# A hybrid encoder layer on one core: sample chunk at full height, paired index heads, low weight parts by an adding DMA, moved stores and fillers

## The chip, the core and the metric

The kernel runs on one core of a Trainium2 chip. Its engines run their own fixed instruction lists side by side and wait for one another through semaphores: TensorE (PE, matmuls; PEld is its weight load), VectorE (DVE), ScalarE (ACT), GpSimd (POOL) and SyncE (SP), which in this kernel issues every DMA before the change. The metric is the device time of one execution in microseconds, the median of the runs shown. Only time counts here; the results must match the reference within its tolerance.

## The reference

One layer of a streaming encoder is computed for two request groups that share all weights: 512 prompt frames and 64 sample frames (576 columns together), model width 1024.

```
mod = silu(c) @ w_ada + b_ada                      # 6 blocks of 1024: shift, scale, gate, twice
h = rms(x) * g * (1 + sc1) + sh1
q,k,v, qi,ki,wi, z, xBC, dt, gates = split(h @ w_in)
# branch A: indexer I[t,s] = sum_h wi[t,h] * relu(qi[t,h] . ki[s] / 8), 8 heads; top k keys; softmax attention
# branch B: causal conv on xBC, chunked scan (SSD, 8 groups of 4 heads), D skip, silu(z) gate, group RMS norm
g_attn, g_ssm = split(sigmoid(gates))
x = x + gt1 * ((g_attn * (oA @ w_branch_attn) + g_ssm * (oB @ w_branch_ssm)) @ w_out)
h2 = rms(x) * g_ffn * (1 + sc2) + sh2
x = x + gt2 * ((silu(gate) * up) @ w_down),   gate, up = split(h2 @ w_gate_up)
```

The sigmoid is computed as (1 + tanh(x / 2)) / 2. New keys, values, conv rows and scan states are outputs too.

## The kernel before, in words

Every product with a weight keeps float32 accuracy with three fast passes. A weight tile of 128 x 1024 numbers (512 KB) is loaded into `raw` (two buffers, `NRAW`), then `split` (line 539) makes a rounded high part `wh` on ACT and the rest, `wl = raw - wh`, on DVE (three buffers of each, `NWH`). The activations have such parts too (`hTh`, `hTl`), and TensorE adds high times high, high times low and low times high. One tile applied to all 576 columns is 48 matmuls of 288 columns. The weight tiles stand in one list, in the order of their use; `fetch` loads and splits them ahead of it, numbered j from 0.

The body `build` doesn't issue instructions; it records operations with their buffers. `Plan.order` (line 363) then lays all of them out with a list scheduler: each operation has a cost from `cost` (line 316) and a priority (its place in the program, shifted by `R.prio`), and for each engine the next ready operation of best priority is taken. What comes out is one fixed order for each engine, SP's DMA issues among them. All instructions are therefore recorded under one line of the profile, L490 (line 490 emits them), and are told apart by the names of their tiles.

The stages, in order:

- Start: `x` is loaded (`xt`), normalised and transposed (`xnT`), while modulation blocks 0 to 3 of `w_ada` (`ada_pair`, tiles `adr`) give shift and scale. `h_tile` makes `hTh` and `hTl`. A second set of transposes makes `xs`, a copy of x in the other layout, stored to `x_d` and read again only after the output projection (lines 815 to 832).
- Small columns: `misc` (index keys, head weights `wi`, dt), the `e` chain of softplus for dt, cumulative sums `acs`.
- Index (line 1090): for each block of query rows, `kis` and `qis` give a score for each head, ACT applies relu (tile `lg`), DVE adds it up with the head's weight (`score`), then picks the top keys with 16 or 18 rounds of `max` and `match_replace`. The sample block (64 rows) runs 8 heads times two halves of 288 keys.
- Attention, for each of 4 key heads: logits `S` (`kst`, `qst`), softmax `P`, its transposes, the values (`pth`, `ptl`, `vst`). Between them TensorE runs fillers: 32 weight tiles of the gate and z columns that need nothing but `h`. `FILL` (line 612) says how many are recorded after each key head, `FILL0` how many before the first. A gate filler applies tanh, then `sg * 0.5 + 0.5` on DVE, and stores it to `gate_d`.
- SSD (line 1383): for each of 8 groups four weight tiles of x, B, C, a conv on DVE and ACT, then four prompt chunks of 128 steps and one sample chunk of 64. In `chunk`, `dec` (decay times CB) and `xdt` (dt times x) give the inside of the chunk and `cs` with the state `st` (tile `hst`) the outside; both add into halves of the array, 64 columns each, chosen by `tile_position` (line 1294). Modulation blocks 10 and 11 (`ada`, tiles `adr`, four loads of 512 KB each) are computed in the last group.
- Branch projections with their gates, modulation blocks 4 to 9 on DVE (`ada_columns`, `aacc`), output projection with `residual` and its gate `gt1`, the FFN by a Strassen-like scheme, the down projection.

```
        vec.tensor_tensor(lo, raw, hi.bitcast(F32), OP.subtract)          # split
    FILL = [6, 5, 5, 4]
            sync.dma_start(x_d[:, :, tb // 2, tb % 2 * P:tb % 2 * P + P], st)
            pe.matmul(o, xdt[:L, 64 * h:64 * h + 64], dec[:L, h, :L], start=True, stop=st is None,
                      tile_position=(0, 64 * (h % 2)))
                ada(10 + i, sd, 2)                                        # in group 7, i = 0 and 1
```

Of the kernel before, what the change touches and what calls it, by code (L numbers as in the profile page):

```python
# [9 lines left out]
OP = mybir.AluOpType  # L10
# [158 lines left out]
class Op:  # L169
    __slots__ = ("eng", "fn", "args", "kw", "dur", "dur_dma", "deps", "succ", "left", "prio", "pools", "t0", "t1", "i", "bytes", "mm", "slack", "port")  # L170
# [58 lines left out]
class Plan:  # L229
# [10 lines left out]
    def __init__(self, tc):  # L240
        self.tc, self.nc = tc, tc.nc
        self.ops, self.events, self.offset, self.slack = [], [], 0, SLACK
        self.vec, self.act, self.pool, self.pe, self.sync = (Engine(self, e) for e in ("vector", "scalar", "gpsimd", "tensor", "sync"))
# [21 lines left out]
    def add(self, eng, fn, args, kw):  # L265
        op = Op()
        op.eng, op.fn, op.args, op.kw = eng, fn, args, kw
        op.i, op.succ, op.pools, op.bytes, op.mm = len(self.ops), [], set(), 0, False
        op.prio = op.i - self.offset
        outs = [args[0] if args else kw["out"]]  # L270
        if kw.get("accum_out") is not None:
            outs.append(kw["accum_out"])
        outs = [o for o in outs if isinstance(o, View)]
        ins = [a for a in list(args[1:]) + [v for k, v in kw.items() if k not in ("out", "accum_out")] if isinstance(a, View)]
        deps = {}
        for v in ins:
# [6 lines left out]
        op.port = eng == "gpsimd" and wide > 0 or eng == "vector" and wide > 1  # L283
        op.dur, op.dur_dma = self.cost(op, outs, ins)
        self.ops.append(op)
        return op
# [29 lines left out]
    def cost(self, op, outs, ins):  # L316
# [10 lines left out]
        if e == "tensor":  # L327
# [8 lines left out]
            if op.kw.get("tile_position") is not None:  # L336
                return (73 if o.shape[0] <= 32 else 8 + n) / 1e3, 0.10
            return ((4 * max(n, 128) / 2.4 if n > 1 else 190) + 5) / 1e3, 0.10
        psum = any(is_psum(v) for v in ins)
# [23 lines left out]
    def order(self):  # L363
# [18 lines left out]
        def enable(op):  # L382
# [4 lines left out]
            t = 0.0  # L387
# [26 lines left out]
        while n < len(ops):  # L414
# [32 lines left out]
            if best == "sync":  # L447
                queue = max(at, queue) + 0.46
                dma_free = max(queue + 1.3, dma_free) + op.bytes / 360e3
                op.t1 = dma_free + op.dur_dma  # L450
            else:
                op.t1 = at + op.dur
# [45 lines left out]
def build(tc, I, O):  # L498
# [40 lines left out]
    def split(raw, nk, n):  # L539
# [5 lines left out]
        vec.tensor_tensor(lo, raw, hi.bitcast(F32), OP.subtract)  # L545
# [19 lines left out]
    def fetch(done, limit=1 << 30):  # L565
# [6 lines left out]
        with R.prio(4000 if done or limit > 99 else 0):  # L572
            more = True
            while more:
                more = False
                j = state["ld"]
                if j < min(len(queue), limit) and j < state["sp"] + NRAW:
# [6 lines left out]
                    else:  # L584
                        raws[j] = (load_raw(*s), s[1], s[2])
# [26 lines left out]
    FILL = [6, 5, 5, 4]  # L612
# [206 lines left out]
    with R.prio(-1500):  # L819
        for tb in range(5):  # L820
# [115 lines left out]
    def fillers(n, pl=None, bufs=2):  # L936
        for nf in range(len(nfs), len(nfs) + n):
            nfs.append(nf)
            if nf == 1 and n == NE:
# [8 lines left out]
                vec.tensor_scalar(sg, sg, 0.5, 0.5, op0=OP.mult, op1=OP.add)  # L948
# [3 lines left out]
            with R.prio(4000):  # L952
# [3 lines left out]
                if nf < 16:  # L956
                    vec.tensor_scalar(sg, sg, 0.5, 0.5, op0=OP.mult, op1=OP.add)
# [19 lines left out]
    vec.tensor_scalar(wi, misc[:, :, 64:72], float(NIH ** -0.5), None, op0=OP.mult)  # L977

# [111 lines left out]
    for b in (4, 1, 2, 3):  # L1090
# [5 lines left out]
        for h in range(NIH):  # L1096
            q0 = 8 * NP_ + h * NS if smp else h * NP_ + b * P
            q = qis[:, q0:q0 + rows]
            for c0, cn in (((0, TH), (TH, TH)) if smp else ((0, n),)):
                ps = px(f"pix{b}_{h}_{c0}", "py")  # L1100
                for a in range(2):
                    pe.matmul(ps[:rows, :cn], q, kis[:, a, k0 + c0:k0 + c0 + cn], start=(a == 0), stop=(a == 1))
                r = ap_.tile([P, NP_], F32, name=f"relu{b}_{h}_{c0}", tag="lg", bufs=4)
                sv = s[:rows, c0:c0 + cn]
                act.activation(r[:rows, :cn], ps[:rows, :cn], AF.Relu, scale=float(HD ** -0.5))
                if h == 0:
                    vec.tensor_scalar(sv, r[:rows, :cn], wi[:rows, b, h:h + 1], None, op0=OP.mult)
                else:
                    vec.scalar_tensor_tensor(sv, r[:rows, :cn], wi[:rows, b, h:h + 1], sv, op0=OP.mult, op1=OP.add)
        if not smp:  # L1110
# [151 lines left out]
    def chunk(g, c, xb, st):  # L1262
# [7 lines left out]
        dec = sd.tile([P, 4, P], F32, name=nm + "dec", tag="dec", bufs=2)  # L1270
# [10 lines left out]
        xdt = sd.tile([P, 256], F32, name=nm + "xdt", tag="xdt", bufs=2)  # L1281
# [42 lines left out]

    xbs, sts = {}, {}
# [57 lines left out]
    for g in range(NG):  # L1383
# [11 lines left out]
        for i in range(4):  # L1395
# [7 lines left out]
            if g == NG - 1 and i < 2:  # L1403
                ada(10 + i, sd, 2)
# [12 lines left out]
    for a in range(8):  # L1417
# [3 lines left out]
        with R.prio(4000):  # L1421
            vec.tensor_tensor(t2(g), ps, t2(g), OP.mult)
# [16 lines left out]
    for a in range(8):  # L1439
# [5 lines left out]
        vec.tensor_tensor(t2(g), ps, t2(g), OP.mult)  # L1445
# [28 lines left out]
    def residual(a, ps, hf, last):  # L1474
        x = x2[a][:, hf]
        for s, c0, n in SEG:
            vec.scalar_tensor_tensor(x[:, c0:c0 + n], ps[:, c0:c0 + n], gt1[:, a, s:s + 1], x[:, c0:c0 + n], op0=OP.mult, op1=OP.add)
# [16 lines left out]
    vec.tensor_scalar(gt2h, gt2, 0.5, None, op0=OP.mult)  # L1494
    for hf in range(2):
# [275 lines left out]
```

## Time and profile before

| | |
|---|---|
| runs, us | 1444.67, 1446.85, 1447.4 |
| median, us | 1446.85 |
| profiled execution, us | 1454.0 |
| its span, first to last instruction, us | 1452.3 |
| mean granted TensorE clock | 0.993 |

The profile is of one execution. Times are microseconds from the start of the span. "Busy" of an engine is the time in which one of its instructions ran; for PE the ends of pipelined matmuls are modelled, so the pace is better read from the distance of starts. A group's row has the busy time and the mean of one instruction, a window's row the busy time of each engine in a stretch. In a timeline or a wait table, the bracket or the arrow names how long the engine stood idle and what ended it. A matmul in plain float32 shows as two rows, one in the fast three-pass form as one.

### The profile page before, as it was taken

Reading aid. Unit: us, or ns where it says so; the run is one execution under the profiler, and the core shown is the slowest. Engines: PE = TensorE matmul, PEld = TensorE weight load, DVE = VectorE, ACT = ScalarE, POOL = GpSimd, SP = SyncE. Lnnn points to the kernel's source line nnn. Section 1 sums busy time; section 2 is a strip of 40 time slices with the busy share of each in tenths; the row PEclk is TensorE's granted clock in tenths of the full one; section 3 lists DMA queues with packets and bytes.
Section 4 is the critical chain, followed back from the end, with each engine's and each line's share of the span. In section 5 each row is a group of like instructions: output and inputs, shape, how many; then the busy total and the mean of one; then the engine's idle time right before and its main releaser. Section 6 shows DMA issues by size and latency. Waiting matters only on the chain.

```text
span 1452.3 us, 27797 instructions
## 1 busy us (share of the span) xinstructions
PE 1415.3 (97%) x10865; PEld 1339.4 (92%) x10865; DVE 1078.2 (74%) x2123; ACT 705.2 (49%) x1482; POOL 211.1 (15%) x320
## 2 busy tenths in 40 slices
PE   7999999999999899999999899999999999999998
PEld 5889999999999699999998699999999999999998
DVE  4468999887877777778777578984699888874221
ACT  5335233556556656555555441123566666663221
POOL 1211001210200144444444210000000000000000
PEclk9999999999999999999999999999999999999999
DMA  9822346333332434344333857775513333324331
GB/s 281 227 73 76 84 112 163 94 84 89 109 92 77 129 99 108 100 112 111 84 88 96 280 171 238 230 229 170 165 44 102 88 99 92 102 70 137 112 107 28
DMA packets 262356, 179.73 MB, mean 124 GB/s; under 512 B 24272, under 2 KB 239472, under 8 KB 262224
## 3 DMA queue, kind: packets, MB, share of 16 engines
q1 hardware_dynamic: 262224, 177.95, 42.7%
q8 instruction: 85, 1.39, 0.4%
q14 instruction: 47, 0.39, 0.1%
HBM read 153.09 MB, written 24.83 MB: 123 GB/s over the span
## 4 chain that ended last, share of the span: by engine, by line
PE 84%; DVE 8%; DMA 5%; SPq 1%; ACT 1%; issue 1%; DVEq 0%; ACTq 0%
PE mm L490 60%; PE py L490 15%; PE px L490 8%; DMA adr<-in_w_ada 2%; DMA raw<-in_w_in 2%; DVE aacc L490 1%; SPq L490 1%; DVE wl L490 1%; DVE m L490 1%; DVE score L490 1%; DMA xt<-in_x_sample 1%; ACT wh L490 0%; DMA x2r<-x_d 0%; DVE P L490 0%; DVE e L490 0%
## 5 line engine op out<-in xcount | busy, mean ns | idle before, releaser
L490 ACT ACTIVATE wh<-raw 128x1024 fp32r<-128x1024 f32 (+2 forms) x159 | 156.6, 987 | 279.9 <-PE mm L490 222.4
L490 DVE TENSOR_TENSOR wl<-raw,wh 128x1024 fp32r<-128x1024 f32 (+1 forms) x137 | 169.0, 1236 | 100.6 <-ACT wh L490 97.8
L490 PE MATMUL mm<-hTl,wh 128*128 128x288 f32 (+1 forms) x1024 | 235.0, 304 | 0.0
L490 PE MATMUL mm<-hTh,wh 128*128 128x288 f32 (+1 forms) x1024 | 230.6, 302 | 1.7 <-ACT xc L490 1.5
L490 PE MATMUL mm<-hTh,wl 128*128 128x288 f32 (+1 forms) x1024 | 232.1, 301 | 0.0
L490 PEld LDWEIGHTS mm<-hTh,wh 128*128 128x128 f32 (+1 forms) x1024 | 166.7, 189 | 5.4 <-ACT xc L490 1.8
L490 PEld LDWEIGHTS mm<-hTl,wh 128*128 128x128 f32 (+1 forms) x1024 | 167.4, 189 | 4.0 <-issue 1.9
L490 PEld LDWEIGHTS mm<-hTh,wl 128*128 128x128 f32 (+1 forms) x1024 | 167.3, 189 | 2.7 <-issue 0.5
L490 DVE SCALAR_TENSOR_TENSOR cu<-xc,wc,cu 128x579 f32<-128x579 f32 x96 | 82.9, 868 | 4.0 <-ACT cu L490 3.5
L490 PE MATMUL mm<-fl,wh 128*128 128x288 f32 x352 | 80.6, 298 | 1.0 <-DVE fl L490 1.0
L490 PE MATMUL mm<-fh,wl 128*128 128x288 f32 x352 | 80.1, 298 | 0.9 <-DVE x2r L490 0.9
L490 PE MATMUL mm<-fh,wh 128*128 128x288 f32 x352 | 80.0, 297 | 0.0
L490 PE MATMUL mm<-wh,hTl 128*128 128x256 f32 x256 | 73.2, 286 | 0.0
L490 PE MATMUL mm<-wh,hTh 128*128 128x256 f32 x256 | 72.8, 286 | 0.0
L490 PE MATMUL mm<-wl,hTh 128*128 128x256 f32 x256 | 72.7, 284 | 0.0
L490 DVE SCALAR_TENSOR_TENSOR aacc<-adr,sil,aacc 128x512 f32<-128x512 f32 x84 | 58.7, 747 | 2.9 <-DMA adr<-in_w_ada 2.7
L490 ACT ACTIVATE P<-lg,mn 128x128 f32<-128x128 f32 (+4 forms) x72 | 41.8, 582 | 39.1 <-DVE mn L490 38.3
L490 PEld LDWEIGHTS mm<-fh,wl 128*128 128x128 f32 x352 | 58.2, 189 | 1.6 <-DVE x2r L490 1.4
L490 PEld LDWEIGHTS mm<-fl,wh 128*128 128x128 f32 x352 | 58.2, 189 | 1.6 <-DVE fl L490 1.4
L490 PEld LDWEIGHTS mm<-fh,wh 128*128 128x128 f32 x352 | 58.1, 189 | 0.1
L490 PE MATMUL mm<-yh,wl 128*128 128x288 f32 x256 | 56.8, 302 | 0.0
L490 PE MATMUL mm<-yh,wh 128*128 128x288 f32 x256 | 56.5, 300 | 0.0
(409 smaller groups left out, 3771.0 us busy)
## 6 DMA issues: line engine op xcount, KB each, us to landing
raw<-in_w_in SPq DMA_DIRECT2D x80, 512.0 KB, 4.2
adr<-in_w_ada SPq DMA_DIRECT2D x48, 512.0 KB, 5.2
rawu<-in_w_gate_up SPq DMA_DIRECT2D x22, 512.0 KB, 3.9
raw<-in_w_gate_up SPq DMA_DIRECT2D x22, 512.0 KB, 3.9
bc<-acs_d SPq DMA_DIRECT2D x32, 256.0 KB, 3.6
raw<-in_w_branch_ssm SPq DMA_DIRECT2D x16, 512.0 KB, 4.9
raw<-in_w_down SPq DMA_DIRECT2D x16, 512.0 KB, 3.7
gate_d<-sg SPq DMA_DIRECT2D x16, 288.0 KB, 4.8
```

The costliest lines, as they stand in the source:

```text
L490: getattr(engines[x.eng], x.fn)(*[real(a) for a in x.args], **{k: real(v) for k, v in x.kw.items()})
```

## The change

Seven edits, made together:

1. Sample chunk: its `dec` and `xdt` get buffers of their own, `decS` and `xdtS`, whose rows 64 to 127 are set to zero once. The matmul reads all 128 rows in every chunk.
2. Index, sample block: heads 2h and 2h+1 stand beside each other in `qis`, so one matmul serves both, with 128 rows of result. Relu, weight and sum run on 128 rows, for 4 pairs. `wi2` holds the weights in that layout. At the end ACT copies the odd half, and DVE adds it.
3. Weight tiles j = 24 to 78 (from the fillers after the first key head to the last but one of the SSD): `wl` is written by ACT as minus `wh`, and a DMA issued by POOL adds `raw` onto it.
4. The store of `xs` is held back in the plan by 60 us.
5. The gates stay tanh: no `sg * 0.5 + 0.5`; the merge computes (g + 1) times the product, and `gt1h`, half of `gt1`, takes up the factor.
6. `FILL` is 5, 5, 5, 5. Modulation blocks 10 and 11 are recorded in SSD groups 2 and 3.
7. The planner's costs: an adding DMA has a price, sync transfers a lower rate, matmuls with a tile position 132 ns.

```diff
@@ order, add
+        op.hold = self.hold
-            t = 0.0
+            t = op.hold
@@ split
+        if not by_dma:
+            vec.tensor_tensor(lo, raw, hi.bitcast(F32), OP.subtract)
+        else:
+            act.activation(lo, hi.bitcast(F32), AF.Copy, scale=-1.0)
+            pool.dma_start(lo, raw, accum_op=OP.add)
@@ fetch
-                        raws[j] = (load_raw(*s), s[1], s[2])
+                        raws[j] = (load_raw(*s), s[1], s[2], 24 <= j < 79)
@@
-    FILL = [6, 5, 5, 4]
+    FILL = [5,5,5,5]
@@ x_d
+            R.hold = 60.0
             if tb < 4:
                 sync.dma_start(x_d[:, :, tb // 2, tb % 2 * P:tb % 2 * P + P], st)
...
+            R.hold = 0.0
@@ fillers (twice)
-                vec.tensor_scalar(sg, sg, 0.5, 0.5, op0=OP.mult, op1=OP.add)
@@ index
-        for h in range(NIH):
-            q0 = 8 * NP_ + h * NS if smp else h * NP_ + b * P
-            q = qis[:, q0:q0 + rows]
+        for h in range(NIH // 2 if smp else NIH):
+            q0 = 8 * NP_ + h * P if smp else h * NP_ + b * P
+            q = qis[:, q0:q0 + P]
+            w1 = wi2[:, h:h + 1] if smp else wi[:, b, h:h + 1]
...
+        if smp:
+            odd = ap_.tile([P, T], F32, name="odd", tag="lg", bufs=4)
+            act.activation(odd[0:NS], s[NS:P, :], AF.Copy)
+            vec.tensor_tensor(s[0:NS, :], s[0:NS, :], odd[0:NS], OP.add)
@@ chunk
-        dec = sd.tile([P, 4, P], F32, name=nm + "dec", tag="dec", bufs=2)
+        dec = decS if c == 4 else sd.tile([P, 4, P], F32, name=nm + "dec", tag="dec", bufs=2)
-        xdt = sd.tile([P, 256], F32, name=nm + "xdt", tag="xdt", bufs=2)
+        xdt = xdtS if c == 4 else sd.tile([P, 256], F32, name=nm + "xdt", tag="xdt", bufs=2)
-            pe.matmul(o, xdt[:L, 64 * h:64 * h + 64], dec[:L, h, :L], start=True, stop=st is None,
+            pe.matmul(o, xdt[:, 64 * h:64 * h + 64], dec[:, h, :L], start=True, stop=st is None,
@@ SSD loop
-            if g == NG - 1 and i < 2:
-                ada(10 + i, sd, 2)
+            if g in (2, 3) and i == 0:
+                ada(8 + g, sd, 2)
@@ branch merge (both branches)
-            vec.tensor_tensor(t2(g), ps, t2(g), OP.mult)
+            vec.scalar_tensor_tensor(t2(g), t2(g), 1.0, ps, op0=OP.add, op1=OP.mult)
```

More of the change, by code (lines that the diff above doesn't have):

```diff
@@ L169 @@
 class Op:
-    __slots__ = ("eng", "fn", "args", "kw", "dur", "dur_dma", "deps", "succ", "left", "prio", "pools", "t0", "t1", "i", "bytes", "mm", "slack", "port")
+    __slots__ = ("eng", "fn", "args", "kw", "dur", "dur_dma", "deps", "succ", "left", "prio", "pools", "t0", "t1", "i", "bytes", "mm", "slack", "port", "hold")
 class Pool:
@@ L977, in build @@
     vec.tensor_scalar(wi, misc[:, :, 64:72], float(NIH ** -0.5), None, op0=OP.mult)
+    wi2 = cp.tile([P, 4], F32, name="wi2")
+    for r in range(2):
+        vec.tensor_copy(wi2[64 * r:64 * r + 64], wi[0:NS, 4].rearrange("p (b r) -> p r b", r=2)[:, r])
     ki = misc[:, :, 0:64]
@@ L1323, in build @@
     so_s = O["ssm_sample"][0, 0].rearrange("h p n -> (h p) n").rearrange("(g a p) n -> g p a n", a=2, p=P)
+    decS = sd.tile([P, 4, NS], F32, name="decS")
+    xdtS = sd.tile([P, 256], F32, name="xdtS")
+    pool.memset(decS[NS:P], 0.0)
+    pool.memset(xdtS[NS:P], 0.0)
     xbs, sts = {}, {}
```

36 lines of the change are left out of this document (21 added, 15 removed).

## The prediction

> **What bounds the kernel now.** I read the page first, then the busy time by stage, then the chain of waits and the timeline at the places where TensorE loses time.
>
> ```profile
> span 1452.3 us, 27797 instructions
> PE 1415.3 (97%) x10865; PEld 1339.4 (92%) x10865; DVE 1078.2 (74%) x2123; ACT 705.2 (49%) x1482; POOL 211.1 (15%) x320
> ...
> PE 84%; DVE 8%; DMA 5%; SPq 1%; ACT 1%; issue 1%; DVEq 0%; ACTq 0%
> ```
>
> TensorE is busy for 97% of the span, and 84% of the chain that ends last lies on it. So only two things can shorten this kernel by much: TensorE work taken away, or one of its few gaps closed. The busy time by stage (windows: length, then PE, PEld, DVE, ACT, POOL, granted clock, DMA share, GB/s) shows where the gaps are.
>
> ```profile
> 0.00:36.00 36.00, 26.45 (x275) 20.75 (x276) 17.43 (x43) 18.65 (x33) 5.75 (x20) 0.95 0.92 281
> 36.00:110.00 74.00, 67.18 (x580) 62.94 (x579) 39.21 (x73) 25.99 (x49) 13.71 (x17) 0.98 0.53 149
> 110.00:460.00 350.00, 347.58 (x2574) 334.36 (x2574) 306.37 (x695) 178.08 (x374) 36.83 (x17) 1.00 0.37 100
> 460.00:500.00 40.00, 34.98 (x187) 26.98 (x186) 31.68 (x81) 23.85 (x58) 1.94 (x13) 0.91 0.22 62
> 500.00:797.00 297.00, 296.82 (x2333) 268.66 (x2332) 232.29 (x445) 174.08 (x426) 134.06 (x229) 1.00 0.40 107
> 797.00:815.00 18.00, 13.71 (x139) 10.43 (x139) 9.28 (x18) 7.30 (x16) 2.75 (x4) 0.91 0.87 277
> ```
>
> Length minus PE gives the idle time: 9.6 us in the first load, 6.8 up to 110, 2.4 in index and attention, 5.0 at the end of attention, 0.2 in the SSD, 4.3 at its end. The granted clock drops where TensorE idles: 0.91 of 40 us is 3.6 us more of lost pace, 0.91 of 18 us is 1.6, 0.98 of 74 us is 1.5.
>
> **Start: the copy of x stored later** (6 DMAs). SP's timeline, ACT's, DVE's and PE's:
>
> ```profile
> 43.39 9.27 SPq L490 DMA_DIRECT2D x_d<-xs  x6
> 58.99 1.00 SPq L490 DMA_DIRECT2D raw<-in_w_in  x2
> 60.57 0.23 ACT L490 ACTIVATE alg<-alg 128x32 f32<-128x32 f32 x1 [4.26 <-DMA alg<-in_a_log]
> 54.32 1.23 DVE L490 TENSOR_TENSOR wl<-raw,wh 128x1024 fp32r<-128x1024 f32 x1 [1.97 <-ACT wh L490]
> 55.80 1.23 DVE L490 TENSOR_TENSOR wl<-raw,wh 128x1024 fp32r<-128x1024 f32 x1 [0.25 <-ACT wh L490]
> ...
> 68.82 1.22 DVE L490 TENSOR_TENSOR wl<-raw,wh 128x1024 fp32r<-128x1024 f32 x1 [5.10 <-ACT wh L490]
> 61.16 0.28 PE L490 MATMUL px<-ident,lg 104*64 104x104 f32 x1 [3.10 <-ACT sg L490]
> ...
> PE px L490 <- DVE e L490: 2.5, 1, 2.5
> ```
>
> The stores hold SP for 9.27 us. Behind them in its queue stand the small tables and the next two weight loads (58.99). ACT waits for the table `alg`, and the gate tanh behind it is late: TensorE stands for 3.1 us. The weight lands late, DVE's `wl` at 68.82 waits, and the whole dt chain `e` stands behind that `wl`: TensorE waits 2.5 us more. Moved back, the stores come behind those tables and loads. Expected back: 3.1 + 2.5 and most of the 1.5 of clock, less what the next wait leaves, since SP gains at most 9.27 us and the two raw buffers are only free when DVE's `wl` ends at 55.6 and 57.0, so the loads come some 2 to 3 us earlier, and without the stores beside them. I take 5.5 us, between 2 and 8.3 (idle and clock together). The stores then stand ahead of later weight loads on SP; there the DMA engines are busy for 0.37 of the time and TensorE has the index's matmuls ready, so I cost that at nothing (without that cover up to the same 5.5, hence 0 in the lowest sum below).
>
> **Index heads paired.** 32 matmuls of 288 columns become 16:
>
> ```profile
> L490 PE MATMUL py<-kis,qis 128*64 128x288 f32 x32 | 6.5, 297 | 0.0
> 1158.33 4.83 PE mm L490 x36
> ```
>
> The pace in a steady stretch of the chain is 4.83 / 36 = 134 ns, so 16 x 0.134 = 2.1 us. DVE loses 8 sums and gains one, ACT loses 8 relus and gains a copy; TensorE doesn't wait for them there (2.4 us idle in 350).
>
> **Sample chunk at full height.** PE's timeline, a prompt chunk and a sample chunk:
>
> ```profile
> 814.22 0.45 PE L490 MATMUL py<-dec,xdt 128*64 128x128 f32 x4
> ...
> 815.29 0.70 PE L490 MATMUL py<-xw,bt 128*128 128x256 f32 x2
> 822.01 0.32 PE L490 MATMUL py<-dec,xdt 64*64 64x64 f32 x2
> 822.27 0.33 PE L490 MATMUL py<-cs,hst 128*64 128x64 f32 x2
> 822.53 0.33 PE L490 MATMUL py<-dec,xdt 64*64 64x64 f32 x2
> ...
> 824.07 0.53 PE L490 MATMUL mm<-oh,wl 128*128 128x288 f32 x2
> ```
>
> The prompt chunk does its 16 rows in 815.29 - 814.22 = 1.07 us. The sample chunk, with half the columns, needs 824.07 - 822.01 = 2.06. The difference between them is that `dec` there runs on 64 rows and `cs` on 128, in turn: each pair takes 0.26 us after the other, with nothing beside it. After the change both have 128 rows, and the two column halves can work side by side as in the prompt chunk. The changed program's order shows the 8 matmuls of every sample chunk still together, and none of 64 rows left. The cost then lies between 0.54 (half the columns, half the time) and 1.07 (time set by weight loads, not by columns); the row of the prompt chunk is the nearest, so I take 0.86. Gain: 8 x (2.06 - 0.86) = 9.6 us, between 7.9 and 12.2. The two clearing instructions on POOL come once.
>
> **Fillers 5, 5, 5, 5.** At the end of attention (460 to 500) idle and clock cost 8.6 us. In the old order the last 70 or so matmuls of the last key head stand with no filler between them; in the new one fillers run between them to the last, and 59 filler matmuls more are left for after it. One tile is 48 x 0.134 = 6.4 us of work that can fill. I take 6, between 0 (the chain of softmax is just as late) and 8.6.
>
> **Modulation blocks 10 and 11.** Chain of waits and PE's timeline:
>
> ```profile
> 800.49 6.79 DMA adr<-in_w_ada
> 802.49 0.79 PE L490 MATMUL mm<-oh,wh 128*128 128x288 f32 x4 [1.30 <-ACT oh L490]
> 807.33 1.08 PE L490 MATMUL py<-adr,sil 128*32 128x128 f32 x16 [2.99 <-DMA adr<-in_w_ada]
> ```
>
> Eight loads of 512 KB stand where the attention outputs, gates and branch weights are loaded too (DMA share 0.87). Moved to groups 2 and 3, they meet a share of 0.40. The 2.99 us go, the clock's 1.6 with them; the wait for `oh` may stay. I take 4.5, between 2 and 5.9. On SP the eight loads now stand ahead of weight loads of the SSD: two waits like the 2.99 would eat it all.
>
> **Tanh gates.** DVE loses 16 of these rows, and the merges keep their widths; `gt1h` is one small instruction.
>
> ```profile
> L490 DVE TENSOR_SCALAR sg<-sg 128x576 f32<-128x576 f32 x16 | 7.7, 479 | 6.7 <-ACT sg L490 6.7
> L490 DVE TENSOR_TENSOR wl<-raw,wh 128x1024 fp32r<-128x1024 f32 (+1 forms) x137 | 169.0, 1236 | 100.6 <-ACT wh L490 97.8
> L490 ACT ACTIVATE wh<-raw 128x1024 fp32r<-128x1024 f32 x128 | 135.2, 1059 | 251.9 <-PE mm L490 195.7 <-issue 40.6 <-DMA raw<-in_w_in 12.9
> raw<-in_w_in SPq DMA_DIRECT2D x80, 512.0 KB, 4.2
> o_d<-oT SPq DMA_DIRECT2D x4, 576.0 KB, 3.0
> x_d<-xs SPq DMA_DIRECT2D x4, 512.0 KB, 6.8
> ```
>
> **Low parts by adding DMA.** The new order has 55 of them. DVE loses 55 x 1.236 = 68 us and the 7.7 above; ACT gains 55 x 1.06 = 58. Both are off TensorE's path (DVE 306 of 350 and 232 of 297 us, ACT 178 and 174): by themselves worth nothing, beyond softmax answering sooner, which the fillers' term has. What counts is the weight feed. A raw buffer was held for load (4.2), ACT (1.06) and DVE (1.24), 6.5 us; now for load, two ACT passes and the adding DMA, and POOL and SP hold up what stands behind it (scan state, `dec`, `cs`; weight loads, `bc`). No adding DMA is in the trace. It reads two tiles and writes one, where a load reads one and writes one, so at the load's pace 4.2 x 1.5 = 6.3; at the least 3.0 (the store of a larger tile), at the most 6.8 + 4.2 = 11.0 (the slowest 512 KB row and a load). I take 6.3, which counts from the row nearest in size. Then a buffer turns in 4.2 + 2.1 + 6.3 = 12.6 us, a weight comes each 6.3 with two buffers; at the most each 8.7. TensorE uses one in 6.4 us when it runs tiles back to back, as at the start of the SSD, but on average one in 297 / 32 = 9.3 us there. So the feed holds on average, and is tight in runs of tiles. Loss: 3 us, between 0 and 4 tiles x (8.7 - 6.4) = 9.
>
> By the Trainium skill, page "DMA: Bandwidth & Descriptors", section "Anatomy of one DMA — SWDGE (gpsimd) path", a DMA issued by GpSimd takes about 2.0 us plus bytes over 436 GB/s, an estimate of 3.2 us here. With that the loss would be 0 and the sum 3 us lower. That fit is for plain copies, and no run here shows it yet.
>
> The planner's new costs reshuffle the order of every engine beside all this; where TensorE's idle is now 0.2 to 2.4 us in 300 it can win nothing and lose little, and I cost it at nothing.
>
> **Sum.** 5.5 + 2.1 + 9.6 + 6 + 4.5 - 3 = 24.7 us. Against the profiled execution's 1454.0 that is 1429.3; that execution is 7.15 above the median of 1446.85, and none of the terms depends on it, so the forecast for the median is **1422**. With all upper ends 8.3 + 2.1 + 12.2 + 8.6 + 5.9 = 37.1 it is 1410. With all lower ends and the full loss (0 + 2.1 + 7.9 + 0 + 2 - 9) it is 1444.
>
> **Rivals.**
>
> - *The gaps only move.* Matmul work goes (2.1 + 9.6 = 11.7), but what closes at one place opens at another: late weights hold the softmax tail and the SSD's start, since POOL's queue now has 55 DMAs that wait for ACT. For it: of all that SP waits for, DVE's `wl`, which frees a raw buffer, is the most, and there are still two raw buffers. Against it: idle in the SSD is 0.2 us in 297, with much slack on DVE and ACT. Time: 1446.85 - 11.7 = 1435. Chance 0.2.
>
> ```profile
> SPq L490 <- DVE wl L490: 494.1, 106, 23.4
> ```
>
> - *The pad does nothing.* If the 0.26 us of a pair comes from 64-column weight loads, not from the turn between 64 and 128 rows, 9.6 falls out: 1432. Against it: the prompt chunk's rows are of the same height and width of weights and run at half that. Chance 0.08.
> - *Weights starve (slower).* One mechanism: the adding DMA takes long enough that two raw buffers no longer feed TensorE. The point: 55 tiles, each (x - 9.3) late, eat the other 27.7 us at x = 9.8 us per weight, a buffer turn of 19.6, an adding DMA of 13.3. That is over twice my value and 2.3 above the dearest bound. At 16 us the turn is 22.3, the loss 55 x 1.85 = 102, the time 1446.85 - 27.7 + 102 = 1521; at 14, 1465. For it: every byte passes three times, beside loads and stores at 0.4 of the DMA engines. Against it: 512 KB rows of 3.0 to 6.8. Chance 0.1, at 1465.
>
> A rule speaks for this last one: the page "SBUF — State Buffer", section "SBUF: two separate sides", of the Trainium skill says that GpSimd can't write the entries of such a DMA while VectorE holds the port that they share, and a short DMA that took 0.62 us took 3.1 so. No run here shows it; 2.5 us more would leave the feed below the point.
>
> **How the numbers follow.** Forecast 0.62, with a range of its own of 1411 to 1433; gaps move 0.2; pad 0.08; starved 0.1. The first three are faster. A difference under 0.2% (2.9 us, the spread of the three runs being 2.7) can't be told from none. From the edge of the second I give 0.03 to no change: faster 0.87, same 0.03, slower 0.10. The range leaves out the starved case and about a tenth of the rest: 1408 to 1441.
>
> **What would show it.** Right: `py<-decS,xdtS` rows at under 0.9 us for a chunk; no 9 us of `x_d` stores ahead of the tables; PE idle near 2 us at the end of attention and at the SSD's end; `wl` landing 5 to 8 us after its issue by POOL. Wrong: PE waiting for a DMA into `wl` again and again, idle in the SSD above 10 us, or stores of x meeting the loads of the key and value weights.

## The result, and the profile after

| | before | after |
|---|---|---|
| median, us | 1446.68 | 1434.92 |
| runs, us | 1444.67, 1446.51, 1446.85, 1447.4 | 1429.4, 1434.5, 1435.34, 1436.43 |
| profiled execution, us | 1454.0 | 1434.5 |

A fourth run of the kernel before moves its median from 1446.85 to 1446.68. The ratio is 0.9914, with a 95% interval of 0.9886 to 0.9942: 12 us less, about half of the 24.7 us that the sum gave. The two profiled executions differ by 19.5 us, because that of before lies 7 us above its median; so stages are compared here for where they idle, and only runs for what a part is worth.

First the page of the changed kernel (busy time and share of each engine), then nearly the same stretches as before (length, then busy PE, PEld, DVE, ACT, POOL, granted clock, DMA share, GB/s).

```profile
span 1432.8 us, 27816 instructions
...
PE 1397.5 (98%) x10849; PEld 1330.7 (93%) x10849; DVE 1014.0 (71%) x2048; ACT 752.5 (53%) x1530; POOL 244.2 (17%) x377
```

```profile
0.00:36.00 36.00, 23.98 (x244) 18.62 (x248) 16.47 (x41) 17.03 (x31) 5.72 (x20) 0.95 0.91 270
36.00:110.00 74.00, 71.64 (x635) 67.20 (x635) 38.28 (x78) 29.85 (x60) 14.77 (x17) 0.98 0.56 154
110.00:440.00 330.00, 327.45 (x2428) 315.27 (x2427) 267.82 (x658) 195.45 (x391) 57.11 (x41) 1.00 0.55 137
440.00:500.00 60.00, 56.19 (x403) 53.97 (x402) 35.16 (x76) 39.02 (x84) 10.32 (x34) 0.99 0.68 175
500.00:797.00 297.00, 289.67 (x2386) 259.21 (x2387) 210.99 (x418) 192.00 (x437) 138.43 (x243) 0.98 0.66 159
797.00:815.00 18.00, 18.00 (x145) 15.70 (x145) 15.52 (x32) 9.30 (x21) 7.93 (x8) 0.93 0.80 271
```

Read length minus PE again. The last row idles nothing, because the SSD ends earlier here: TensorE's wait for `adr` (2.99 us) is gone, but that for `oh`, 1.30 us before, stays and now ends at 794.4 us, in the row above (TensorE's table of waits: what it waited for, us in total, times, longest).

```profile
PE mm L497 <- ACT oh L497: 1.6, 1, 1.6
```

In 36 to 110 us 2.4 us are idle instead of 6.8, but the first 36 us idle 12.0 instead of 9.6. The stretch of 500 to 797, most of the SSD, idled 0.2 us in 297 and now idles 7.3, at a clock of 0.98 instead of 1.00 (another 0.02 x 297 = 6 us of lost pace). The DMA share there rose from 0.40 to 0.66: the weight tiles pass through the DMA engines once more.

The gap at the end of attention is gone too, though the row of 440 to 500 doesn't say so: its 3.8 us are one later wait, which the same table names.

```profile
PE px L497 <- DVE xb L497: 5.0, 2, 3.8
PE px L497 <- DVE hst L497: 3.5, 3, 2.0
```

`xb` is the convolution's result and `hst` the scan state; both belong to the SSD, which so idles 3.8 + 7.3 = 11.1 us from 490 to 797. No row names a DMA into `wl`. The chain of waits, over the stretch that ends at the longest one, shows why (start, us, what; the second fence is a line of ACT's timeline):

```profile
473.66 7.31 DMA wl<-raw
480.97 0.02 SPq L497
...
481.02 8.02 DMA raw<-in_w_in
...
490.02 0.86 ACT cu L497
...
499.19 0.70 DVE xb L497
...
499.93 0.79 PE px L497 x2
```

```profile
489.06 1.06 ACT L497 ACTIVATE wh<-raw 128x1024 fp32r<-128x1024 f32 x1 [4.26 <-DMA raw<-in_w_in]
```

An adding DMA takes 7.31 us. Until then its raw buffer is in use, and SP can't issue the next weight load. That load takes 8.02 us, where the median of its kind is 4.2. On ACT the next instruction is `wh` of that weight, for which ACT stands idle for 4.26 us, and `cu`, the first pass of the convolution, stands behind it in the fixed order. So a late weight shows up as a late `xb`. In the SSD TensorE never waits for the weight itself.

What else the weight load met is in SP's timeline: right behind it stand the first two loads of a modulation block. The program before issues the first of them at the start of its SSD too (second fence; a load goes out as soon as its buffer is free, long ahead of its use), so it is the adding DMA that is new there. That it is the cause is argued here; the run with an eighth of its bytes, below, tests it.

```profile
481.02 0.37 SPq L497 DMA_DIRECT2D raw<-in_w_in  x1
481.44 1.58 SPq L497 DMA_DIRECT2D adr<-in_w_ada  x2
```

```profile
497.18 0.49 SPq L490 DMA_DIRECT2D adr<-in_w_ada  x1
```

The sample chunk did what it was to do. From the first of its 16 rows (8 matmuls in plain float32; some records are missing here) to the next work it needs 600.07 - 599.46 = 0.61 us instead of 2.06 (TensorE's timeline):

```profile
599.46 0.27 PE L497 MATMUL py<-cs,hst 128*64 128x64 f32 x1
599.47 0.27 PE L497 MATMUL py<-decS,xdtS 128*64 128x64 f32 x1
...
599.86 0.28 PE L497 MATMUL py<-cs,hst 128*64 128x64 f32 x2
600.07 0.70 PE L497 MATMUL py<-xw,bt 64*128 64x256 f32 x2
```

And the price of the adding DMA, from the DMA table (last number: median us from issue to landing) and the groups of instructions; the last row is of the kernel before:

```profile
wl<-raw POOLq DMA_DIRECT2D x55, 512.0 KB, 5.1
...
L497 POOL DMA_DIRECT2D wl<-raw x55 | 48.7, 886 | 221.1 <-ACT wl L497 159.4 <-PE py L497 27.0 <-ACT pth L497 18.7
L497 ACT ACTIVATE wl<-wh 128x1024 fp32r<-128x1024 f32 x55 | 58.2, 1061 | 0.2
L497 DVE SCALAR_TENSOR_TENSOR cu<-xc,wc,cu 128x579 f32<-128x579 f32 x96 | 91.9, 958 | 27.3 <-ACT cu L497 25.9
...
L490 DVE SCALAR_TENSOR_TENSOR cu<-xc,wc,cu 128x579 f32<-128x579 f32 x96 | 82.9, 868 | 4.0 <-ACT cu L490 3.5
```

The median of 5.1 us lies below the 6.3 that I took, and above the 3.2 of the fit on the page "DMA: Bandwidth & Descriptors", section "Anatomy of one DMA — SWDGE (gpsimd) path", of the Trainium skill; the measurement decides. DVE's `cu`, which had waited 4.0 us in all before (mean 868 ns), now waits 27.3 us, and takes 958 ns.

At this point my theory was: the gain is TensorE's work (pad and index) and the closed gaps, less 7 us and more in the SSD, lost because ACT's 55 additional passes push `cu` back.

### The profile page after: what moved, and what is told of

Its sections match the earlier page's. It is cut to its first block, busy times and chain, and to the rows that moved or that the text cites. A ratio compares the mean times of both kernels' runs of the same rounds, so it can differ in the third digit from the quotient of the medians.

```text
span 1432.8 us, 27816 instructions
## 1 busy us (share of the span) xinstructions
PE 1397.5 (98%) x10849; PEld 1330.7 (93%) x10849; DVE 1014.0 (71%) x2048; ACT 752.5 (53%) x1530; POOL 244.2 (17%) x377
## 4 chain that ended last, share of the span: by engine, by line
PE 84%; DVE 8%; ACT 2%; DMA 2%; issue 2%; POOL 1%; SPq 0%; ACTq 0%; DVEq 0%; POOLq 0%
PE mm L497 60%; PE py L497 15%; PE px L497 9%; DVE score L497 1%; DVE wl L497 1%; DVE m L497 1%; DVE cu L497 1%; DVE aacc L497 1%; DMA adr<-in_w_ada 1%; ACT wh L497 1%; DVE yl L497 1%; DMA raw<-in_w_in 1%; DMA wl<-raw 1%; DVE xb L497 0%; DVE tok L497 0%
## 5 line engine op out<-in xcount | busy, mean ns | idle before, releaser
L497 PE MATMUL mm<-hTh,wh 128*128 128x288 f32 (+1 forms) x1024 | 235.1, 305 | 1.7 <-ACT hTh L497 1.7
L497 PE MATMUL mm<-hTh,wl 128*128 128x288 f32 (+1 forms) x1024 | 235.4, 305 | 0.6 <-DVE wl L497 0.6
L497 PE MATMUL mm<-hTl,wh 128*128 128x288 f32 (+1 forms) x1024 | 231.8, 302 | 0.3 <-DVE hTl L497 0.3
L497 DVE TENSOR_TENSOR wl<-raw,wh 128x1024 fp32r<-128x1024 f32 (+2 forms) x82 | 98.8, 1207 | 79.0 <-ACT wh L497 76.2
L497 DVE SCALAR_TENSOR_TENSOR cu<-xc,wc,cu 128x579 f32<-128x579 f32 x96 | 91.9, 958 | 27.3 <-ACT cu L497 25.9
L497 POOL DMA_DIRECT2D wl<-raw x55 | 48.7, 886 | 221.1 <-ACT wl L497 159.4
L497 ACT ACTIVATE wl<-wh 128x1024 fp32r<-128x1024 f32 x55 | 58.2, 1061 | 0.2
```

The costliest lines, as they stand in the source:

```text
L497: getattr(engines[x.eng], x.fn)(*[real(a) for a in x.args], **{k: real(v) for k, v in x.kw.items()})
```

## The experiments

Each kernel was timed in five rounds beside the kernel before. "Worth" below is (1 - ratio) x 1446.68 us. In the diffs, `...` stands for lines left out here.

| run | kernel | median, us | ratio to before | 95% interval |
|---|---|---|---|---|
| (the change) | after | 1434.92 | 0.9914 | 0.9886 to 0.9942 |
| e1_no_dma | after, no adding DMA | 1428.07 | 0.9859 | 0.9833 to 0.9885 |
| e2_pad_only | before, pad alone | 1439.18 | 0.9938 | 0.9912 to 0.9965 |
| e3_hold_only | before, later stores alone | 1441.39 | 0.9955 | 0.9937 to 0.9973 |
| e4_dma_only | before, adding DMA alone | 1443.13 | 0.9967 | 0.9952 to 0.9983 |
| e5_dma_attention | after, adding DMA up to weight 47 | 1423.11 | 0.9833 | 0.9819 to 0.9848 |
| e6_act_pass | after, ACT's pass kept, DVE adds | 1441.38 | 0.9959 | 0.9946 to 0.9972 |
| e7_fill_ada | before, fillers and blocks alone | 1452.95 | 1.0044 | 1.0025 to 1.0062 |
| e8_no_hold | after, stores not held | 1432.39 | 0.9904 | 0.9887 to 0.9921 |
| e9_small_add | after, adding DMA of an eighth of the partitions | 1428.64 | 0.9866 | 0.9841 to 0.9892 |
| e10_old_fill | e5 with the fillers of before | 1419.72 | 0.9809 | 0.9785 to 0.9832 |
| e11_old_ada | e5 with the blocks in the last group | 1418.79 | 0.9802 | 0.9778 to 0.9825 |
| e12_both_old | e5 with both as before | 1418.78 | 0.9797 | 0.9778 to 0.9816 |

**No adding DMA.**

```diff
-                        raws[j] = (load_raw(*s), s[1], s[2], 24 <= j < 79)
+                        raws[j] = (load_raw(*s), s[1], s[2])
```

> The changed kernel, but every low part is made by DVE's subtraction, none by an adding DMA. Theory (the adding path's extra ACT passes, 55 x 1.06 us, stand ahead of the convolution's ACT work, so that xb and the scan state are late and TensorE idles 7.3 us in the SSD instead of 0.2): the SSD's idle falls below 2 us, ratio to the kernel before about 0.986 (1427 us), 6 to 9 us better than the changed kernel. Rival 1 (the adding path frees DVE, and that is what closed the gaps of attention): 0.995 or worse, with the gap at the end of attention back at 4 to 5 us. Rival 2 (the path is neutral, the missing gain is at the start): 0.991, as the changed kernel.

1428.07 us, 8 us better than the changed kernel: the adding DMAs cost more in sum than they win. The windows of this kernel, from its attention tail to its SSD, and TensorE's longest wait there:

```profile
443.00:500.00 57.00, 52.52 (x355) 48.82 (x353) 41.53 (x92) 35.27 (x85) 6.29 (x24) 0.97 0.40 121
500.00:785.00 285.00, 283.21 (x2402) 256.86 (x2400) 233.69 (x443) 170.18 (x412) 136.39 (x221) 1.00 0.42 113
```

```profile
PE px L497 <- DVE xb L497: 3.4, 1, 3.4
```

The gap of 4.5 us before the SSD is back, so rival 1 has a part in it. The 1.8 us of idle time in the SSD are the first half of one wait of 3.4 us for `xb`, from 783.2 to 786.6, which the end of the window cuts. So a late `xb` comes without any adding DMA too, and less of the SSD's loss goes with them than 7.3 - 1.8: from 490 to 815 us this kernel idles 4.6 us and the changed one 11.2. Which part of the path hurts this run doesn't say.

**The pad alone.**

```diff
+        dec = decS if c == 4 else sd.tile([P, 4, P], F32, name=nm + "dec", tag="dec", bufs=2)
...
+        xdt = xdtS if c == 4 else sd.tile([P, 256], F32, name=nm + "xdt", tag="xdt", bufs=2)
-            pe.matmul(o, xdt[:L, 64 * h:64 * h + 64], dec[:L, h, :L], start=True, stop=st is None,
+            pe.matmul(o, xdt[:, 64 * h:64 * h + 64], dec[:, h, :L], start=True, stop=st is None,
...
```

> The kernel before with the sample chunk's decay and input tiles padded to 128 rows, nothing else. Theory (11.1 us of TensorE work are taken away and nothing else moves): 0.9923 (1435.6 us), with the chunk's 16 rows at 0.66 us. Rival (gaps only move: TensorE waits elsewhere in the SSD for what the sample chunk's slowness hid): 0.996 or worse, idle in the SSD above 3 us. Rival of the pad (the time comes from 64-column weights, not from the turn between 64 and 128 rows): 16 rows stay at 2 us, 1.000.

Worth 9.0 us (5 to 13), against 8 x 1.45 = 11.6 from the rows above. TensorE's timeline and the window of the SSD in this kernel:

```profile
526.84 0.34 PE L490 MATMUL py<-decS,xdtS 128*64 128x64 f32 x4
...
527.50 0.70 PE L490 MATMUL py<-xw,bt 64*128 64x256 f32 x2
```

```profile
500.00:790.00 290.00, 287.85 (x2370) 263.09 (x2369) 236.17 (x447) 176.71 (x434) 131.49 (x227) 1.00 0.40 107
```

The chunk takes 0.66 us, so the rival of the pad falls. Of the other something is seen: 2.1 us idle in the SSD instead of 0.2, which is most of the difference between 11.6 and 9.0 (within the interval there need be none).

**The later stores alone.**

```diff
+            R.hold = 60.0
             if tb < 4:
...
+            R.hold = 0.0
```

> The kernel before with only the stores of the x copy planned 60 us later. My prediction's own term: 5.5 us, 0.9962 (1441.2 us). Theory now (the gap behind the tables closes, but the ada loads and the weights come no sooner, so the start's end hardly moves): 0.998 to 1.000, and the wait for alg gone from ACT's rows. Rival (the changed kernel's profile had a late start by chance): 0.996 with the first index matmul 5 us earlier.

Worth 6.5 us (4 to 9), so my theory of this run was wrong, and the prediction's 5.5 right. Its window from 36 to 110 us against the 6.8 us idle of before:

```profile
36.00:110.00 74.00, 73.14 (x641) 68.92 (x640) 41.94 (x85) 32.34 (x65) 14.91 (x17) 1.00 0.54 148
```

0.9 us idle, and the clock at 1.00 instead of 0.98.

**The adding DMA alone.**

```diff
+            act.activation(lo, hi.bitcast(F32), AF.Copy, scale=-1.0)
+            pool.dma_start(lo, raw, accum_op=OP.add)
...
-                        raws[j] = (load_raw(*s), s[1], s[2])
+                        raws[j] = (load_raw(*s), s[1], s[2], 24 <= j < 79)
...
```

> The kernel before with the adding DMA for the weights 24 to 78 and the planner's costs for it, nothing else. Theory (the SSD loses about 8 us to late conv results, attention wins a little from the freed DVE): 1.003 to 1.006 (1451 to 1455 us), idle in the SSD 5 to 10 us, waits of TensorE for xb and the scan state. Rival 1 (the freed DVE closes the attention gap and the SSD loss needs the other edits): 0.996 to 0.999. Rival 2 (neutral): 1.000. If weights starved, TensorE would wait for the DMA into wl: I expect no such row above 2 us.

4.8 us faster (2 to 7), where I expected slower: rival 1. The windows of this kernel, attention's end and the SSD:

```profile
450.00:490.00 40.00, 38.31 (x269) 36.06 (x268) 23.76 (x54) 26.80 (x59) 7.62 (x22) 1.00 0.65 165
490.00:780.00 290.00, 287.88 (x2255) 257.86 (x2255) 205.65 (x410) 190.76 (x432) 137.27 (x247) 1.00 0.65 153
```

At the end of attention it idles 1.7 us at full clock, where before it was 5.0 at 0.91, with the old fillers. So it is the adding path that closes that gap, not fillers. DVE's freed time is the likely reason: it is busy for 24 of those 40 us, where before it was 32. But this kernel has another order too, and no run parts the two. In the SSD it idles 2.1 us, less than my 5 to 10, and does 2255 matmuls in 290 us (7.78 a us) where before did 2333 in 297 (7.86): some 3 us lost by this rough count, since the two stretches mix the matmuls differently, and no starving.

**ACT's second pass without the DMA.**

```diff
             act.activation(lo, hi.bitcast(F32), AF.Copy, scale=-1.0)
-            pool.dma_start(lo, raw, accum_op=OP.add)
+            vec.tensor_tensor(lo, raw, lo.bitcast(F32), OP.add)
```

> The changed kernel where ACT still writes the negated high part (its second pass of 1.06 us stays), but DVE adds the raw weight to it in place of the adding DMA; so POOL issues nothing for it and DVE has its 55 passes back. Theory (ACT's extra pass ahead of the conv's ACT work makes the SSD late): the SSD still idles 5 us or more, 0.991 or worse. Rival (the DMA itself, its issue on POOL and its landing 5.1 us later, makes it late): the SSD's idle below 2 us, 0.987 or better.

The time fits my theory, but the place is wrong. The windows of this kernel, attention's end and the SSD:

```profile
460.00:508.00 48.00, 39.69 (x200) 29.94 (x199) 32.34 (x79) 27.84 (x64) 4.40 (x20) 0.89 0.29 88
508.00:785.00 277.00, 276.06 (x2332) 248.78 (x2332) 223.38 (x428) 185.87 (x430) 118.77 (x217) 1.00 0.42 116
```

In the SSD ACT is as busy as in the changed kernel (186 us in 277, against 192 in 297), and TensorE idles 0.9. So ACT's passes by themselves do not delay the SSD, in the order that this kernel has: the theory falls there. With DVE loaded again, and its subtraction now behind two ACT passes, attention idles 8.3 us at a clock of 0.89.

**The adding DMA in attention only.**

```diff
-                        raws[j] = (load_raw(*s), s[1], s[2], 24 <= j < 79)
+                        raws[j] = (load_raw(*s), s[1], s[2], 24 <= j < 48)
```

> The changed kernel with the adding DMA kept for the weights 24 to 47 (used in index and attention) and DVE's subtraction for the rest (SSD). Theory (the path helps in attention, where DVE is busy for 306 of 350 us, and hurts in the SSD): the best of these kernels, 0.984 to 0.987 (1424 to 1428 us). Rival (it hurts or is neutral in both): no better than the same kernel without any adding DMA. Rival (the SSD's loss is from other edits): 0.991 with the SSD's idle still above 5 us.

1423.11 us: 11.7 us better than the changed kernel (0.9914 - 0.9833), 3.8 better than with no adding DMA at all (though these two intervals overlap a little). The first 210 us from the SSD's start show it: of the changed kernel, then of this one.

```profile
490.00:700.00 210.00, 203.01 (x1692) 181.26 (x1692) 144.53 (x287) 137.32 (x311) 96.47 (x177) 0.98 0.71 172
```

```profile
490.00:700.00 210.00, 210.00 (x1793) 189.98 (x1792) 169.19 (x320) 124.78 (x302) 97.63 (x163) 1.00 0.44 119
```

7.0 us idle and 0.02 x 210 = 4.2 us of lost pace in one, nothing in the other: about 11 of the 11.7 us, given a clock of two digits. In the 100 us after them the two idle nearly alike, 4.2 and 3.2 us. This kernel has an order of its own, so these 11.7 us are the adding DMAs of the SSD together with the order laid out for them.

**The stores not held.**

```diff
-            R.hold = 60.0
+            R.hold = 0.0
```

> The changed kernel with the stores of the x copy planned where they were. My prediction's term: 5.5 us worse than the changed kernel, 0.9952. Theory now (the start won nothing, its gap moved to the next late load): 0.991 within 0.0015, with the 9 us of stores back ahead of the tables and TensorE's wait for sg back.

0.9904, the same as the changed kernel. Its SP timeline, one line of the changed kernel's for comparison (second fence), and its window:

```profile
47.51 5.06 SPq L497 DMA_DIRECT2D x_d<-xs  x4
54.64 0.35 SPq L497 DMA_DIRECT2D cs<-in_rope  x1
...
61.90 0.37 SPq L497 DMA_DIRECT2D raw<-in_w_in  x1
...
64.48 1.51 SPq L497 DMA_DIRECT2D x_d<-xs  x2
```

```profile
54.23 0.34 SPq L497 DMA_DIRECT2D cs<-in_rope  x1
```

```profile
36.00:110.00 74.00, 71.95 (x638) 67.30 (x637) 39.53 (x79) 30.41 (x61) 15.83 (x17) 0.98 0.55 155
```

I had expected the stores and the wait back; instead the plan puts two of the six behind the weight loads by itself, and 2.0 us idle, about as in the changed kernel (2.4). The other four still stand ahead of the tables (`cs`, the first of them), but they end at 52.57, before the tables go out. Without them, in the changed kernel, the tables go out at 54.23 all the same, where the kernel before had 52.76. So the stores no longer hold the tables, and the edit is worth nothing beside the other edits. Which of those delays the tables was not tried.

**Fillers and modulation blocks alone.**

```diff
-    FILL = [6, 5, 5, 4]
+    FILL = [5, 5, 5, 5]
-            if g == NG - 1 and i < 2:
-                ada(10 + i, sd, 2)
+            if g in (2, 3) and i == 0:
+                ada(8 + g, sd, 2)
```

> The kernel before with only the fillers 5, 5, 5, 5 and the two modulation blocks moved into groups 2 and 3. My prediction's terms: 6 + 4.5 = 10.5 us, 0.9927 (1436.3 us). Theory now (both gaps close): 0.991 to 0.995, with idle below 2 us at the end of the SSD and below 3 at the end of attention. Rival (the closing of attention's gap in the changed kernel came from DVE freed by the adding DMA, not from the fillers): 0.997, the attention gap still 4 us or more.

6.4 us slower (4 to 9), where prediction and theory had it faster. The windows of this kernel, end of attention and end of the SSD:

```profile
460.00:504.00 44.00, 37.24 (x169) 26.49 (x168) 32.35 (x95) 25.86 (x66) 1.11 (x10) 0.84 0.14 40
...
800.00:815.00 15.00, 12.23 (x92) 10.95 (x91) 11.92 (x21) 8.69 (x18) 2.75 (x6) 0.98 0.50 132
```

At the end of attention 6.8 us idle and 0.16 x 44 = 7.0 lost in pace make 13.8, against 8.6 before (in 40 us). One filler tile fewer after the first key head did not help the last one: TensorE still waits there for the parts of the softmax (`pth` 2.0 us, `mn` 1.1, `P` 0.9). At the end of the SSD 2.8 us idle instead of 4.3, with hardly any loss of clock.

**An eighth of the adding DMA, all else in place.**

```diff
-            pool.dma_start(lo, raw, accum_op=OP.add)
+            pool.dma_start(lo[:16], raw[:16], accum_op=OP.add)
```

> The changed kernel with every instruction in the same place on every engine, but each of the 55 adding DMAs treats 16 of the 128 partitions, an eighth of the bytes. Left out: the other 112 partitions of these low parts, so they hold the negated high part and the products are not the reference's. It divides what the adding path costs in the SSD. Theory (the transfer itself: its bytes beside the other DMAs, its landing of 5.1 us, its hold on DVE's rows): TensorE's idle in the SSD falls from 7.3 to below 3 us, DVE's cu rows from 0.98 to 0.90 us or less, time 1427 to 1430 us, as the kernel without adding DMAs in the SSD. Rival 1 (POOL's queue: 55 issues of 0.886 us and their waits for ACT, which an eighth of the bytes keeps): idle stays at 6 us or more if the issue time stays near 0.9 us, 1433 to 1436 us. Rival 2 (the order that the planner makes for it): the same, 1433 to 1436 us, even where the issue gets shorter.

Neither clean case. The time is that of the theory (1428.64), the idle time of the SSD is not. The rows of this kernel: landing, POOL's issue, DVE's `cu`, a wait of TensorE, and the same 210 us of the SSD.

```profile
wl<-raw POOLq DMA_DIRECT2D x55, 64.0 KB, 3.2
...
L497 POOL DMA_DIRECT2D wl<-raw x55 | 43.0, 781 | 220.7 <-ACT wl L497 163.0 <-PE py L497 29.1 <-ACT pth L497 18.9
L497 DVE SCALAR_TENSOR_TENSOR cu<-xc,wc,cu 128x579 f32<-128x579 f32 x96 | 92.6, 965 | 24.0 <-ACT cu L497 22.7
...
PE px L497 <- DVE hst L497: 3.3, 3, 1.9
...
490.00:700.00 210.00, 206.85 (x1747) 184.97 (x1746) 147.23 (x295) 138.90 (x313) 94.87 (x182) 0.99 0.51 127
```

Landing falls from 5.1 to 3.2 us only, POOL's issue from 886 to 781 ns. The idle time of the 210 us falls from 7.0 to 3.2 us: the 3.8 us wait for `xb` at the SSD's start is gone, with every instruction in its place, so it was the bytes of the adding DMAs that made it. (The wait for `xb` that is left, 1.15 us at the SSD's end, the changed kernel has too.) From 500 to 797 us, the stretch that I had named, it idles 7.2 us and the changed kernel 7.3. So what goes with the bytes is that one wait and some pace (a clock of 0.99 for 0.98). The waits for the scan state `hst` stay, 3.3 us against 3.5. So of the 11.7 us, some 7 (0.9914 - 0.9866) go with the bytes and the landing, those in attention among them; 5 (0.9866 - 0.9833) stay with POOL's issues, ACT's passes or the order laid out for them. The intervals on both sides overlap a little, so the split is rough. DVE's `cu` stays at 965 ns and its wait at 24 us: the bytes are not what slows it. Nor are ACT's passes: where they were kept without the DMA, `cu` waits 3.0 us in all. It waits 21 to 28 us in the four kernels with all 55 adding DMAs and 2.6 to 4.1 in the ten others, so POOL's issues or the order are left.

**The old fillers in the best kernel.**

```diff
-    FILL = [5,5,5,5]
+    FILL = [6, 5, 5, 4]
```

> The kernel with adding DMAs for the weights 24 to 47 (1423.1 us) with the fillers of before, 6, 5, 5, 4. My prediction's term: the fillers are worth 6 us, so 1429 us, a gap of 4 us back at the end of attention. Theory now (in the kernel before, the new fillers and modulation blocks together lost 6.5 us, and its attention lost 8): the new fillers are worth nothing or less: 1418 to 1423 us. Rival (they cost only where DVE is full, and help where it is freed): 1426 us or more.

Its four runs, 1418.87 to 1420.69 us, all lie below the four of the kernel with the new fillers (1421.82 to 1423.36): 3.5 us by the ratios. But the two were timed in different sets of runs, and the ratios' intervals overlap (0.9785 to 0.9832 against 0.9819 to 0.9848), so by itself this gain is not clear of the noise.

**The old place of the blocks in the best kernel.**

```diff
-            if g in (2, 3) and i == 0:
-                ada(8 + g, sd, 2)
+            if g == NG - 1 and i < 2:
+                ada(10 + i, sd, 2)
```

> The same kernel (1423.1 us) with the modulation blocks 10 and 11 back in the last group. My prediction's term: 4.5 us, so 1427.6 us, with TensorE's wait for adr of some 3 us back at the end of the SSD. Rival (moving them only shifts 2 x 16 matmuls and 8 loads into the SSD, whose own idle grows as much): 1423 us within 1.5. Rival (they disturb the SSD's weight feed): 1421 us or less.

4.5 us better (the two intervals just touch, 0.9778 to 0.9825 and 0.9819 to 0.9848), so the move costs time here. The gap that it was to close doesn't come back: TensorE waits at the end of the SSD (700 to 850 us) for `oh` alone in this kernel, and longer, and for two tiles more, in the one with the blocks moved (second fence).

```profile
PE mm L497 <- ACT oh L497: 1.9, 1, 1.9
```

```profile
PE mm L497 <- ACT oh L497: 2.5, 1, 2.5
PE px L497 <- DVE xb L497: 0.4, 1, 0.4
PE px L497 <- DVE hst L497: 0.3, 1, 0.3
```

That is 1.3 us of the 4.5; the rest is spread over the stages, and I found no one place for it.

**Both.** The two edits above together.

> The changed kernel with adding DMAs for the weights 24 to 47 alone, the fillers of before (6, 5, 5, 4) and the modulation blocks 10 and 11 in the last group as before: that is, without the parts that cost time one by one. If the two gains add (3.4 us for the fillers and 4.3 us for the blocks below 1423.1): 1415 to 1416 us, ratio 0.978. If both let the same late thing go: 1418 to 1420 us, 0.981.

1418.78 us, the same as either alone: they don't add. With both, the gain over the kernel with adding DMAs up to weight 47 is 5.2 us and clear of the noise. This version beats both kernels, 2.0% below the kernel before, with an interval of 1.8 to 2.2.

## Why the prediction was half right

The direction held, and so did the outer range of 1408 to 1441; the size did not. 1434.92 lies outside the forecast's own range, 1411 to 1433, and on the time of the rival to which I gave 0.2. That the outer range held was in part luck: three terms had the wrong sign or came to nothing, and gains whose source is open filled in. By its own steps:

- **Sample chunk at full height, 9.6 us.** Right. 2.06 us became 0.61, nearer to the low bound of 0.54 than to the 0.86 that I took; 9.0 us in runs alone. "The pad does nothing" is refuted.
- **Index pairs, 2.1 us.** Not tried alone; the rows did fall from 32 to 16.
- **The copy of x stored later, 5.5 us.** Right by itself (6.5), and worth nothing in the changed kernel. What failed is that "the planner's new costs reshuffle the order of every engine" was costed at nothing. With the other edits in place the stores move partly by themselves, the tables go out no sooner without the rest of them, and the first 36 us idle 12.0 us instead of 9.6. All nine kernels here that start from the changed one idle 11.8 to 12.1 us there, the five that start from the kernel before 9.1 to 10.2. So neither the pad, the stores, the adding DMA with its price nor the fillers and blocks do it alone. Of what is left (pairs, gates, the planner's other prices) none was tried; my guess is the lower rate for sync transfers, since that stretch is made of loads.
- **Fillers, 6 us, and modulation blocks, 4.5 us.** Wrong in sign, and the largest miss of the sum: +10.5 became a loss. Together they lose 6.4 us alone and 5.2 in the best kernel, where the parts (3.5 and 4.5) are less sure. I read the attention gap as a lack of fillers, but it stays with the new fillers and closes with the adding path. For the blocks, I charged a wait for `adr` to their place, but with the other edits it is gone in the old place too; and "they meet a share of 0.40" was the share of before, while the adding DMAs of the same change made it 0.66. That is not why the move costs time, though: it does so also where the share is 0.43 or 0.44. Why is open.
- **Low parts by adding DMA, -3 us, bounds 0 and -9.** The size, 8.0 us lost in the changed kernel, lies within the bounds; the reasons failed. Its DMA time was about right (5.1 for 6.3). Two things were missing. First, DVE's freed time is not "worth nothing" beside the fillers: alone, the edit is 4.8 us faster. Second, the feed "holds on average", but TensorE is not who feels it: ACT's order puts the convolution behind `wh` of the next weight, so one turn of 7.31 + 8.02 us delays `xb`. In the SSD the DMAs with their order cost 11.7 us; in index and attention they win 3.8, though that interval overlaps. My sign of being wrong, over 10 us idle in the SSD, came true with the 11.1 us above.
- **Tanh gates, 0.** Not tried alone. The kernel with no adding DMA is 20.4 us faster than before, though its fillers and blocks lose by themselves; pad and index (its 2.1 us an estimate) explain 11 to 14 of it, and up to 110 us it idles 14.7 us instead of 16.4. What closed the rest, DVE's time saved by gates and index or the new order, is open.
- **The sum.** The parts don't add. The four tried alone are worth 9.0 + 6.5 + 4.8 - 6.4 = 13.9 us; taken out of the changed kernel or of the better one, the same parts give other values, the adding DMA and the stores above all. So no sum of single terms accounts for the 12 us. And "none of the terms depends on it", of the 7.15 us by which the profiled execution was slow, does not hold for the clock losses in the terms (3.6 + 1.6 + 1.5): runs of the kernel before on record show a mean granted clock of 0.995 to 0.998 at 1443 us and of 0.992 to 0.995 at 1450.

Of the rivals, "the gaps only move" (chance 0.2, 1435) names the time that came out and half the mechanism: a late weight did hold the SSD's start. It did not hold the softmax tail, whose gap closed. "Weights starve" did not come: no wait of TensorE for a DMA into `wl`. Its sentence from the page "SBUF — State Buffer", section "SBUF: two separate sides", of the Trainium skill finds no support here: one landing took 7.31 us beside a median of 5.1, in a stretch full of other DMAs, and no run here separates the port from that.

My theory after the result, that ACT's passes push `cu` back, fell with the run that kept them. What remains open is the last 5 us of the SSD's loss, between POOL's issues, ACT's passes together with them, and the order. The waits for `hst` are the part of it that is seen: 3.5 us in the changed kernel, 3.3 with an eighth of the bytes, 0.3 without adding DMAs in the SSD. They don't come with the adding DMA alone in the kernel before, so the order has a part in them.

## What to carry to other kernels

Before costing a slower feed, look whose queue holds the instruction that consumes it: work that stands behind it in the same fixed order is late too, and the trace will blame that work. An edit that uses a free resource, here the DMA engines at 0.40, must be costed with the share that the change itself leaves (0.66, and one weight load of 8.02 us against a median of 4.2), not with that of the profile before. Take a change apart even if it wins: here the adding DMAs of the SSD, and the fillers with the blocks, cost time, and leaving them out took the gain from 0.9 to 2.0%.

## What the runs showed that I had not expected

An eighth of the bytes of an adding DMA lands after 3.2 us, the whole after 5.1, and its issue holds POOL for 0.78 us instead of 0.89: most of its price doesn't depend on its size. The 16 rows that alternate between 64 and 128 rows of the array cost 2.06 us, and 0.61 us at 128 throughout, though the latter multiply more. And a gap costs more than its length, because the granted clock is lower beside it, but by no fixed rate: at the end of attention 0.84 in 44 us with 6.8 idle in one kernel and 0.96 in 40 us with 6.2 idle in another (before with the pad alone).
